# A planner's 512-column working tiles raised from 40 to 47, in room taken from the DMA scratch

## The chip, the cores and the metric

The kernel runs on one core of one Trainium2 chip. The time is the device time of one execution in microseconds. Before the change three runs took 2082.89, 2094.52 and 2097.59 us, a median of 2094.52 us.

## The reference

Two models run one after the other, all in float32, batch 1 and model width 1024, on 256 tokens.

The first model has two layers and a context of 256 further tokens. Each layer begins with a modulation: a vector `silu(c) @ ada_w + ada_b` of six parts that shift, scale and gate. The even layer (layer 0) mixes with multi-head attention of eight heads beside gated linear attention in chunks of 64. The odd layer (layer 1) mixes with a gated delta network of eight heads: chunks of 64 tokens, forward and backward, and in each chunk a triangular system is solved.

```
a_mat = jnp.where(strict, jnp.einsum('bhnid,bhnjd->bhnij', kb, k) * decay, 0.0) + jnp.eye(C)
sol = lax.linalg.triangular_solve(a_mat, rhs, left_side=True, lower=True)
...
s = s * ge_c[..., None, None] + jnp.einsum('bhcd,bhcv->bhdv', ke_c, v_new)
```

After each mixer comes an MLP with squared ReLU, of inner width 4096. The second model has two hybrid layers (sparse attention over a chosen set of keys, beside an mLSTM), each followed by a gated MLP of inner width 2816. It is modulated in the same way, from `w_mod`.

## The kernel before

Activations lie in SBUF as tiles with 128 of the model's columns on the partitions and the tokens along the row. Every dense product is done three times on TensorE: the weights and the activations are split into a high part and a low rest, and high by high, high by low and low by high are added in PSUM. Weights come in pieces of 128x1024 (512 KB, eight blocks of 128x128) through `Stream.piece` (line 694): one DMA from SP's queue into `wraw` (4 buffers), then `whi` by ScalarE or VectorE and `wlo` always by VectorE (3 buffers each). A dense product of 512 columns over the model width is 24 matmuls, one piece. Modulation weights come as `mraw` (512 KB each, 4 buffers); a group of eight program matmuls `modps` (16 in the trace, since each makes two passes) uses two of them.

The order of all instructions is not the order of the code. The class `Program` records every operation with the tiles that it reads and writes, and `schedule` (line 460) then plays the engines forward with costs written in the class, and hands each engine the operation of the highest priority that is ready. An operation that opens a tile may start only when its group of tiles has a free slot: `fits` (line 516) asks `Slots.room` (line 242), and this also keeps slots back for tiles that earlier operations will need. Four groups hold the working tiles, by their length in columns, and the last one, of 512 columns (2 KB on each partition), has `H2` slots:

```
for size, bufs in ((4, 64), (64, 24), (256, self.H1), (512, self.H2)):
    if n <= size:
        return self.nc.tile(self.act, shape, dtype, name, f"t{size}", bufs)
```

So `H2` bounds how far the plan can run ahead in any layer. Where TensorE would have nothing to do, or only narrow matmuls, the planner puts in matmuls `filled`, which compute nothing that is used (lines 416 and 591 to 608). They are the only instructions whose number depends on the plan. Some operations may go to either of two engines, and the planner chooses.

The constants `cst` of a layer are loaded into 512-column slots too (`load_consts`, line 757; `cst_1130`, `1132`, `1133` for layer 1, `cst_2230`, `2231`, `2232` for the second model) and hold them until their last use.

Layer 1 is the place that the prediction speaks of most. In `odd_layer` (line 1224) it holds the normalised input, split, in 16 slots of 512 columns (`xnh`, `xnl`), keys in 8 (`kT`, `kN`), queries in 2 and values in 8 (`vN`). A value product (eight of them) passes through `conv3`, which takes up to three slots more (`cy`, `cc`, `ce`), and then four transposes `vT`. Beside it `gdn_inverse` (line 1567) brings the triangular matrices (`N`) through DRAM (`gscr`) into a tile `inv`, inverts half blocks there by a recursion of 30 steps on VectorE (`invt`, `inv`), and writes them to DRAM again (`inv<-inv`). `gdn_rows` (line 1630) reads them back as `YY`, and with its first matmul, `iw`, the scan over the chunks begins.

Of the kernel before, what the change touches and what calls it, by code (L numbers as in the profile page):

```python
# [714 lines left out]
class Kernel:  # L715
# [3 lines left out]
    CV, CQ = range(6), ()  # L719
    PINP = range(4)  # L720
    EARLY = (1500, 1000, 500, 300)
    H2, H1, H0 = 40, 12, 4

    def __init__(self, tc, A, out, vat, cat):
        self.tc, self.nc, self.A, self.out, self.vat, self.cat = tc, Program(tc), A, out, vat, cat
# [1402 lines left out]
```

## Time and profile before

| | |
|---|---|
| median of three runs | 2094.52 us |
| the profiled execution | 2076.82 us |
| its span, first to last instruction | 2074.9 us |
| TensorE busy | 1994.3 us, 96% |
| weight loads busy | 1660.5 us, 80% |
| VectorE busy | 1440.4 us, 69% |
| ScalarE busy | 777.2 us, 37% |
| GpSimd busy | 261.3 us, 13% |
| mean granted clock of TensorE | 0.99 |
| moved by DMA | 328.16 MB, mean 158 GB/s |

The profile is of one execution. Busy time counts overlapping instructions of an engine once; matmuls are pipelined and their ends are modelled. A wait is put down to the event that came last before the waiting instruction started.

### The profile page before, as it was taken

The numbers are of one execution on the slowest core, as the hardware profiler recorded it, in microseconds if no ns is written. First come the engines' busy times: TensorE is split into PE (matmuls) and PEld (weight loads), VectorE is DVE, ScalarE is ACT, GpSimd is POOL, SyncE is SP. The second block draws the span as 40 slices with busy tenths as digits, with TensorE's granted clock in tenths as the row PEclk, the third lists the DMA queues.
The fourth block names the chain that finished last, engine by engine and source line by source line (L and its number), as shares of the span: only waits on it lengthen the run. The fifth ranks groups of instructions, "written<-read, shape, count | busy, mean of one in ns | idle before, by whom it ended". The sixth has DMA issues, their size and how long they took to land.

```text
span 2074.9 us, 37880 instructions
## 1 busy us (share of the span) xinstructions
PE 1994.3 (96%) x15248; PEld 1660.5 (80%) x15248; DVE 1440.4 (69%) x2959; ACT 777.2 (37%) x1594; POOL 261.3 (13%) x253
## 2 busy tenths in 40 slices
PE   7999999999999999799999999999999989989998
PEld 4766647888888778467889997787899968779998
DVE  5437655655555577757477888987887778878775
ACT  4134552301102266133253225564543155655431
POOL 1001002100000220006121103101200050021001
PEclk9999999999999999899999999999999999999999
DMA  8574103333333427777256567554666633424663
GB/s 326 197 282 141 42 31 127 118 90 96 99 99 95 159 77 159 243 261 215 60 175 208 176 187 259 195 182 157 228 184 186 214 112 108 137 82 150 183 186 102
DMA packets 108444, 328.16 MB, mean 158 GB/s; under 512 B 27211, under 2 KB 28491, under 8 KB 108140
## 3 DMA queue, kind: packets, MB, share of 16 engines
q1 hardware_dynamic: 108268, 325.73, 49.4%
q8 instruction: 120, 1.97, 0.4%
q14 instruction: 56, 0.46, 0.1%
HBM read 320.45 MB, written 5.24 MB: 157 GB/s over the span
## 4 chain that ended last, share of the span: by engine, by line
PE 85%; DVE 6%; ACT 3%; DMA 3%; issue 1%; POOL 0%; DVEq 0%; ACTq 0%; POOLq 0%
PE ps L684 66%; PE modps L684 3%; DMA mraw<-in_mod_dram 3%; PE filled L684 2%; PE po L684 1%; PE sc L684 1%; DVE acc L684 1%; ACT ny L684 1%; DVE fy L684 1%; PE ss L684 1%; PE glao L684 1%; PE as L684 1%; PE gdno L684 1%; PE pt L684 1%; PE ao L684 1%
## 5 line engine op out<-in xcount | busy, mean ns | idle before, releaser
L684 DVE TENSOR_TENSOR wlo<-wraw,whi 128x512 fp32r<-128x512 f32 x796 | 544.4, 713 | 45.7 <-ACT whi L684 34.6
L684 PE MATMUL ps<-xnh,whi 128*128 128x256 f32 (+1 forms) x1696 | 471.1, 317 | 9.4 <-ACT whi L684 3.5
L684 PE MATMUL ps<-xnl,whi 128*128 128x256 f32 (+1 forms) x1696 | 468.9, 316 | 1.2 <-POOL xnl L684 0.6
L684 PE MATMUL ps<-xnh,wlo 128*128 128x256 f32 (+1 forms) x1696 | 469.3, 316 | 0.1
L684 DVE CAST whi<-wraw 128x1024 fp32r<-128x1024 f32 x225 | 155.7, 696 | 346.9 <-PE ps L684 346.3
L684 PEld LDWEIGHTS ps<-xnh,whi 128*128 128x128 f32 x1696 | 302.8, 190 | 41.8 <-issue 6.3
L684 PEld LDWEIGHTS ps<-xnl,whi 128*128 128x128 f32 x1696 | 302.9, 191 | 26.6 <-issue 4.7
L684 PEld LDWEIGHTS ps<-xnh,wlo 128*128 128x128 f32 x1696 | 303.4, 191 | 25.8 <-issue 5.2
L684 ACT ACTIVATE whi<-wraw 128x1024 fp32r<-128x1024 f32 x173 | 182.6, 1058 | 358.1 <-PE ps L684 333.9
L684 POOL TENSOR_TENSOR sq<-sq 128x256 f32<-128x256 f32 (+1 forms) x53 | 56.4, 1064 | 829.6 <-ACT sq L684 769.5
L684 PE MATMUL ps<-mh,wlo 128*128 128x512 f32 (+1 forms) x512 | 139.7, 336 | 0.0
L684 PE MATMUL ps<-mh,whi 128*128 128x512 f32 (+1 forms) x512 | 139.6, 336 | 0.0
L684 PE MATMUL ps<-ml,whi 128*128 128x512 f32 (+1 forms) x512 | 139.1, 336 | 0.0
L684 PE MATMUL filled<-fill 128*128 128x512 f32 x414 | 128.9, 436 | 0.0
L684 PE MATMUL modps<-mraw,cst 128*32 128x256 f32 x1408 | 98.2, 396 | 22.0 <-DMA mraw<-in_mod_dram 12.3
L684 PEld LDWEIGHTS ps<-ml,whi 128*128 128x128 f32 x512 | 89.7, 190 | 10.2 <-DVE ml L684 0.2
L684 PEld LDWEIGHTS ps<-mh,wlo 128*128 128x128 f32 x512 | 89.8, 190 | 9.9
L684 PEld LDWEIGHTS ps<-mh,whi 128*128 128x128 f32 x512 | 89.8, 190 | 10.0
L684 PEld LDWEIGHTS filled<-fill 128*128 128x128 f32 x414 | 76.1, 200 | 26.9 <-issue 13.7
L684 PEld LDWEIGHTS modps<-mraw,cst 128*32 128x32 f32 x1408 | 36.8, 110 | 66.0 <-DMA mraw<-in_mod_dram 21.8
L684 PE MATMUL ps<-fh,whi 128*128 128x256 f32 x352 | 88.3, 284 | 0.0
L684 PE MATMUL ps<-fh,wlo 128*128 128x256 f32 x352 | 87.8, 285 | 0.1
(513 smaller groups left out, 3398.5 us busy)
## 6 DMA issues: line engine op xcount, KB each, us to landing
mraw<-in_mod_dram SPq DMA_DIRECT2D x192, 512.0 KB
wraw<-in_mlp_dram SPq DMA_DIRECT2D x128, 512.0 KB
wraw<-in_gu_dram SPq DMA_DIRECT2D x88, 512.0 KB
wraw<-in_hin_dram SPq DMA_DIRECT2D x54, 512.0 KB
wraw<-in_dn_dram SPq DMA_DIRECT2D x44, 512.0 KB
wraw<-in_oin_dram SPq DMA_DIRECT2D x25, 512.0 KB
wraw<-in_ein_dram SPq DMA_DIRECT2D x18, 512.0 KB
wraw<-in_hout_dram SPq DMA_DIRECT2D x16, 512.0 KB
```

Of the source, the lines that this page charges most:

```text
L684: getattr(self.real[op.eng], method)(*a, **kw)
```

## The change

Two numbers are changed. The program object is made with a DMA scratch of 1 KB on each partition in place of the 16 KB that it has by default, and the seven more slots of 512 columns (14 KB on each partition) go into that room.

```diff
-    H2, H1, H0 = 40, 12, 4
+    H2, H1, H0 = 47, 12, 4
...
-    nc = bacc.Bacc("TRN2", target_bir_lowering=False, num_devices=1)
+    nc = bacc.Bacc("TRN2", target_bir_lowering=False, num_devices=1, dynamic_dma_scratch_size=1024)
```

No operation of the computation is added or removed. The order changes on every engine, since the planner has other slots to give. TensorE's program holds 12244 rows other than fillers both times, and 414 fillers before, 351 now. Counted at the same landmarks of TensorE's program, the fillers up to each are:

| up to the first | before | now |
|---|---|---|
| `logit` (layer 0's gates, end of the first stage) | 23 | 30 |
| `ab` (layer 1's gates) | 81 | 82 |
| `iw` (layer 1's scan) | 172 | 130 |
| dense product of layer 1's output (`oh`) | 230 | 189 |
| `ki` of the first hybrid layer | 254 | 218 |
| `ki` of the second hybrid layer | 335 | 274 |
| end | 414 | 351 |

GpSimd's program grows from 258 to 267 instructions, ScalarE's shrinks from 1532 to 1525 and VectorE's from 2910 to 2908. SP has 671 both times.

The first place is TensorE in layer 1, at the recursion: `qk` and `gT` belong to the scan's preparation, `ps` with 128x512 are dense products for the values, and the recursion itself runs on VectorE beside these rows. Before:

```order
L684 MATMUL filled<-fill 128x512 x11
L684 MATMUL ps<-xnh,whi 128x512
L684 MATMUL ps<-xnl,whi 128x512
L684 MATMUL ps<-xnh,whi 128x512
L684 MATMUL ps<-xnl,whi 128x512
L684 MATMUL filled<-fill 128x512 x11
L684 MATMUL modps<-mraw,cst 32x256 x8
L684 MATMUL filled<-fill 128x512 x3
L684 MATMUL modpt<-cst_80,modsb 128x128 x2
L684 MATMUL modps<-mraw,cst 32x256 x8
L684 MATMUL filled<-fill 128x512 x6
L684 MATMUL modps<-mraw,cst 32x256 x8
```

And now:

```order
L684 MATMUL beR<-be,cst_1131 64x8 x4
L684 MATMUL filled<-fill 128x512 x2
L684 MATMUL ps<-xnh,whi 128x256
L684 MATMUL ps<-xnl,whi 128x256
L684 MATMUL qk<-qT,kT 64x64 x16
L684 MATMUL modps<-mraw,cst 32x256 x8
L684 MATMUL filled<-fill 128x512 x4
L684 MATMUL modpt<-cst_80,modsb 128x128 x2
L684 MATMUL filled<-fill 128x512 x5
L684 MATMUL modps<-mraw,cst 32x256 x8
L684 MATMUL filled<-fill 128x512 x6
L684 MATMUL modps<-mraw,cst 32x256 x8
```

What moved are the value products. Before, 92 of their 128x512 matmuls stand behind the last group `modps` with fillers around it, and now 22; the other 70 stand ahead of the rows shown. Between that group and the first `iw` stood 22 fillers and 12 groups `modps`; now no filler and two groups. By `iw` the plan has run 45 groups in place of 50, by `gdno` (the scan's output) 46 in place of 55. The rest is made up later: between the second hybrid layer's beginning (the last `fh` matmul) and its `ki` stand 10 groups in place of 4.

The second place is SP's queue there (`gscr` takes a matrix to DRAM, `inv<-gscr` brings a half of one back in another layout, `wraw<-in_oin` is a weight piece of layer 1). Before:

```order
L684 DMA wraw<-in_oin_dram 128x1024 x5
L684 DMA gscr<-N 128x512 x2
L684 DMA inv<-gscr 8x64x64 x4
L684 DMA gscr<-N 128x512 x6
L684 DMA wraw<-in_oin_dram 128x1024
L684 DMA inv<-gscr 8x64x64 x12
L684 DMA wraw<-in_oin_dram 128x1024 x4
L684 DMA mraw<-in_mod_dram 128x1024 x16
L684 DMA inv_1333<-inv 64x4096
L684 DMA inv_1332<-inv 64x4096
```

And now:

```order
L684 DMA gscr<-N 128x512 x3
L684 DMA inv<-gscr 8x64x64 x4
L684 DMA gscr<-N 128x512
L684 DMA inv<-gscr 8x64x64 x4
L684 DMA gscr<-N 128x512 x4
L684 DMA wraw<-in_oin_dram 128x1024 x4
L684 DMA inv<-gscr 8x64x64 x8
L684 DMA wraw<-in_oin_dram 128x1024 x2
L684 DMA mraw<-in_mod_dram 128x1024 x2
L684 DMA wraw<-in_oin_dram 128x1024 x2
L684 DMA mraw<-in_mod_dram 128x1024 x2
```

Eight of the sixteen `inv<-gscr` are issued earlier, and four weight pieces stand ahead of the last eight in place of one ahead of the last twelve. Further on, the first `YY` was issued behind six pieces of `oout`, and mod pieces between them; it now follows right behind five pieces of `oin` and four of `oout`.

The third place is SP's queue at the beginning of the program, as a difference:

```order
+L684 DMA cst_1130<-in_cst_dram 128x512
 L684 DMA cst_1131<-in_cst_dram 128x66
-L684 DMA mraw<-in_mod_dram 128x1024 x4
+L684 DMA cst_1132<-in_cst_dram 128x512
+L684 DMA cst_1133<-in_cst_dram 128x512
+L684 DMA cst_2230<-in_cst_dram 128x512
+L684 DMA mraw<-in_mod_dram 128x1024 x2
+L684 DMA cst_2231<-in_cst_dram 128x512
+L684 DMA cst_2232<-in_cst_dram 128x512
+L684 DMA mraw<-in_mod_dram 128x1024 x2
```

Six constants of later layers, 256 KB each, are loaded in the first stage, four of them ahead of modulation pieces that layer 0 begins with. They hold six of the 47 slots from there on; before, four of them were loaded at the end of layer 0's mixer, and two at the end of layer 1's.

## Rows read from the trace of the kernel before

**Rows 1.** The page's head and section 1, whole span: busy us, share, instructions.

```profile
span 2074.9 us, 37880 instructions
...
PE 1994.3 (96%) x15248; PEld 1660.5 (80%) x15248; DVE 1440.4 (69%) x2959; ACT 777.2 (37%) x1594; POOL 261.3 (13%) x253
```

**Rows 2.** Busy time by stretch, all engines: stretch, length, engines' busy (count), clock, DMA, GB/s.

```profile
0.00:50.00 50.00, 35.80 (x335) 23.91 (x336) 27.93 (x63) 23.74 (x45) 8.30 (x9) 1.00 0.89 325
450.00:500.00 50.00, 50.00 (x223) 41.37 (x222) 30.91 (x49) 11.30 (x17) 0.00 (x0) 1.00 0.32 95
820.50:859.80 39.30, 29.94 (x271) 18.77 (x267) 37.43 (x142) 10.81 (x23) 3.00 (x4) 0.91 0.66 240
859.80:945.50 85.70, 74.79 (x616) 55.12 (x616) 47.57 (x84) 32.57 (x81) 11.26 (x11) 0.96 0.85 276
945.50:1024.00 78.50, 76.57 (x2038) 63.33 (x2035) 46.34 (x88) 22.64 (x50) 32.07 (x33) 1.00 0.45 136
1651.60:1693.00 41.40, 34.90 (x242) 25.95 (x240) 29.11 (x51) 19.15 (x46) 19.61 (x25) 0.92 0.44 149
```

**Rows 3.** Costliest groups of the page (its section 5): count, busy us, mean ns, idle before.

```profile
L684 PE MATMUL filled<-fill 128*128 128x512 f32 x414 | 128.9, 436 | 0.0
L684 PE MATMUL modps<-mraw,cst 128*32 128x256 f32 x1408 | 98.2, 396 | 22.0 <-DMA mraw<-in_mod_dram 12.3
```

**Rows 4.** Busy time by stretch of the filler matmuls alone, columns as in Rows 2.

```profile
0.00:736.80 736.80, 28.39 (x81) 16.15 (x81) 1.00 0.41 135
736.80:820.50 83.70, 6.32 (x18) 2.98 (x18) 1.00 0.52 97
820.50:859.80 39.30, 15.32 (x51) 9.73 (x51) 0.91 0.66 240
859.80:945.50 85.70, 6.94 (x22) 3.69 (x22) 0.96 0.85 276
945.50:1045.00 99.50, 17.74 (x58) 9.63 (x58) 1.00 0.38 118
```

**Rows 5.** Instructions on tile inv: count, ns min/median/max, first and last start.

```profile
L684 DVE TENSOR_TENSOR invt<-inv x60: 178/342/739, 828.2 to 857.5; 128x30 f32<-128x30 f32 x4, 128x58 f32<-128x58 f32 x4, 128x84 f32<-128x84 f32 x4, 128x108 f32<-128x108 f32 x4
...
L684 SPq DMA_DIRECT2D inv<-gscr x16: 281/2045/3771, 775.4 to 813.0; - x16
L684 SPq DMA_DIRECT2D YY<-inv x16: 579/626/842, 934.5 to 996.6; - x16
```

**Rows 6.** Timeline of TensorE at 835 us: start, length, instruction, idle before and releaser.

```profile
835.26 0.38 PE L684 MATMUL modpt<-cst,modsb 128*128 128x128 f32 x2
842.46 0.65 PE L684 MATMUL modps<-mraw,cst 128*32 128x256 f32 x4 [6.82 <-DVE mod L684]
```

**Rows 7.** Chain that ended last, 815 to 950 us: start, length, what.

```profile
818.61 8.81 DMA mraw<-in_mod_dram
...
848.32 4.32 DMA mraw<-in_mod_dram
...
853.38 5.73 DMA mraw<-in_mod_dram
...
866.35 12.71 DMA mraw<-in_mod_dram
```

**Rows 8.** Waits of TensorE, 820 to 946 us: us in total, times, longest.

```profile
PE modps L684 <- DVE mod L684: 7.9, 2, 6.8
PE modps L684 <- DMA mraw<-in_mod_dram: 6.9, 4, 5.8
```

**Rows 9.** Chain over the whole span, a piece of 512-column dense matmuls.

```profile
63.85 34.71 PE ps L684 x153
```

**Rows 10.** Busy time by stretch, all engines, four stretches of 7 us.

```profile
835.00:842.00 7.00, 0.64 (x4) 0.28 (x2) 6.97 (x23) 0.00 (x0) 0.74 (x1) 0.88 0.44 150
842.00:849.00 7.00, 6.54 (x42) 3.52 (x43) 6.46 (x23) 0.00 (x0) 0.83 (x1) 0.63 0.49 157
871.00:878.00 7.00, 1.20 (x11) 0.66 (x11) 1.38 (x3) 1.39 (x2) 0.00 (x0) 0.75 0.99 349
878.00:885.00 7.00, 6.81 (x37) 4.22 (x34) 4.51 (x9) 4.84 (x11) 0.00 (x0) 0.76 1.02 400
```

**Rows 11.** Idle time of TensorE ahead of modps: releaser, us in total, times.

```profile
  DMA mraw<-in_mod_dram: 34.1, 31
```

**Rows 12.** Timeline of SP's DMA issues, 770 to 862 us.

```profile
773.29 0.93 SPq L684 DMA_DIRECT2D gscr<-N  x2
775.37 3.92 SPq L684 DMA_DIRECT2D inv<-gscr  x4
779.39 5.31 SPq L684 DMA_DIRECT2D gscr<-N  x6
788.87 0.33 SPq L684 DMA_DIRECT2D wraw<-in_oin_dram  x1
789.30 25.38 SPq L684 DMA_DIRECT2D inv<-gscr  x12
814.78 2.86 SPq L684 DMA_DIRECT2D wraw<-in_oin_dram  x4
818.61 39.02 SPq L684 DMA_DIRECT2D mraw<-in_mod_dram  x16
860.21 1.17 SPq L684 DMA_DIRECT2D inv<-inv  x2
```

**Rows 13.** Waits of SP's queue, 737 to 960 us: us in total, times, longest.

```profile
SPq L684 <- DVE wlo L684: 49.4, 12, 13.5
```

**Rows 14.** Instructions on tile iw, columns as in Rows 5.

```profile
L684 PE MATMUL iw<-YY,N x256: 184/191/212, 943.8 to 1006.3; 32*32 32x32 f32 x128
```

**Rows 15.** DMA queues of the page (its section 3): packets, MB, share of 16 engines.

```profile
q1 hardware_dynamic: 108268, 325.73, 49.4%
q8 instruction: 120, 1.97, 0.4%
q14 instruction: 56, 0.46, 0.1%
```

## The prediction

> **What bounds the kernel now.** I read the page's busy shares first. TensorE is busy for 1994.3 of 2074.9 us, so 80.6 us are idle; no other engine passes 69% but its own weight loads, which run beside it [rows 1]. Next the busy time by stretch, to see where the idle time lies: in an MLP there is none (50.00 of 50.00 us), while the 125.0 us of layer 1 from 820.50 to 945.50 hold 9.36 + 10.91 = 20.3 us [rows 2]. Third the fillers: 414 of them are busy for 128.9 us, 0.311 us each, and inside "busy" [rows 3]. So TensorE could be shorter by at most 80.6 + 128.9 us, and both parts lie in the mixers. In the two stretches of layer 1 stand 73 fillers, 22.3 us [rows 4].
>
> Last, what ends the waits there. From 828.2 to 857.5 us VectorE runs the recursion [rows 5]. TensorE has little to do beside it, and waits 6.82 us for a modulation vector that VectorE writes between two steps [rows 6]. Then, on the chain that ended last, come modulation pieces in flight: 8.81, 4.32, 5.73 and 12.71 us [rows 7]; DMA is 85% busy behind the recursion, at 276 GB/s [rows 2].
>
> The code says why TensorE is short of work there. At the recursion the input (16), keys (8), queries (2) and values (8) hold 34 slots, and constants held 4 of 40: 2 free, and 6 until the second half of the values is opened. A value product wants three. With 47 slots and six constants in them the same count leaves 7, and 11. The order shows the effect: 70 matmuls of 512 columns now stand ahead of the recursion's last mod group.
>
> **The change part by part.** The real work of TensorE is the same, 12244 rows, so the end moves by fillers, by idle time and by clock.
>
> *Fillers.* 63 fewer, at 0.311 us [rows 3]: -19.6 us. By place: 1 more ahead of `ab`, 43 fewer from there to `iw`, 6 more from there to the first `ki`, 25 fewer to the second one's, 2 fewer behind it. If each had stood beside a wait that stays, removing them would be worth 0; I take the whole, since TensorE is the chain nearly everywhere.
>
> *Idle time in layer 1.* Bounds 0 and -20.3 us [rows 2]. 7.9 us are waits for `mod` behind the recursion, and they stay, for two mod banks still end there; 6.9 us are direct waits for `mraw`, and these lose their cause, since two mod groups in place of twelve stand between the recursion and `iw` [rows 8]. I take half, -10.
>
> A second way to the same number: the stretch of 85.7 us loses 70 matmuls at 34.71/153 = 0.227 us [rows 9], 15.9 us; 22 fillers, 6.9 us [rows 4]; and ten mod groups of 16 passes at 98.2/1408 us, 1.1 us each [rows 3], 11 us. That leaves 52 us, 10.9 of them the old idle time. What is only moved comes up elsewhere, under the recursion or later, so this is no second gain; it shows what would fill the idle time.
>
> *Mod groups paid later.* Six more stand between the last `fh` and `ki` of the second hybrid layer, 41.4 us long with 6.5 idle [rows 2]. Their matmuls are in the real work already. Their pieces, 12 of 512 KB, may come late: TensorE lost 34.1 us to `mraw` over 1408/16 = 88 groups [rows 3, 11], 0.39 us each, so six cost 2.3 us. Bounds 0, as DMA is 44% busy there [rows 2], and 12.7, the longest such wait [rows 7]. I take +2.3.
>
> *Constants in the first stage.* Four of 256 KB are now queued ahead of modulation pieces, where DMA is 89% busy at 325 GB/s [rows 2]: 1.05 MB take 3.2 us. The first stage's seven extra fillers (23 to 30 up to `logit`) carry 2.2 us of this in the sum already, so +1.0. Bounds 0 and, with the two further constants, 4.8 - 2.2 = 2.6.
>
> *SP's queue at the recursion.* Eight of sixteen `inv<-gscr` go early, and the last eight stand behind four weight loads. An `inv<-gscr` of the twelve takes 25.38/12 = 2.1 us of the queue [rows 12]; four fewer behind the last `gscr` save 8.5 us. A load on this queue waited 49.4/12 = 4.1 us for a buffer [rows 13]; four cost 16.5. Bounds -8.5 and +8.0 for the recursion's start; I take 0. Behind SP's queue wait the recursion and, through it, `YY` and the scan.
>
> *YY behind nine weight loads.* SP reached the `inv<-inv` at 860.21 [rows 12]. Nine loads at 4.1 us end at about 898, and the first `iw` came 9.3 us after the first `YY` (943.8 against 934.5 [rows 5, 14]). So the scan could begin at about 907. TensorE's own work reaches 860 + 41 to 52 = 901 to 912. The two meet, and I add nothing.
>
> *Other engines.* Nine more instructions on GpSimd and nine fewer on ScalarE and VectorE lie under TensorE (13, 37 and 69% busy [rows 1]): 0. *The scratch.* All of the program's own transfers are issued by SP on the hardware queue; GpSimd issues none [rows 15]. Whether that queue uses the scratch no row shows; I take 0 and keep the other case as a rival. The Trainium skill (DMA: Bandwidth & Descriptors, Terms) says that software-generated descriptors lie in rings in SBUF and that hardware generation hands them straight to the DMA engines. By that rule the cut is free, and the sum stays as it is; no run here shows where the descriptors lie.
>
> Sum: -19.6 - 10 + 2.3 + 1.0 = -26.3 us. The profiled execution took 2076.82 us, 1.9 of them around its span, so it would be 2050.5. The median of the runs is 17.7 us above that execution; I set the difference against the median: 2094.5 - 26.3 = 2068.2. The forecast's own range goes from -44 (all 20.3 us of idle time, two slow-clock dips gone) to -8 (idle time kept, both late bounds in part).
>
> **Rivals.** One per cent, about what a measurement of this kernel can tell from no change, is 20.9 us: faster is below 2073.6, slower above 2115.4.
>
> *The idle time only moves.* The fillers go, and TensorE waits elsewhere as long as before. For it: much of the idle time here hangs on VectorE's recursion. Against it: rows 7 blame loads that the new order spreads out. -19.6 + 3.3: 2078, within 1%. 16%.
>
> *The scan starts no earlier.* If the nine loads ahead of `YY` wait 8 us each, twice the mean [rows 13], `YY` stays at 934 and layer 1 gains nothing. The 20 fillers elsewhere remain: -6.2 + 3.3, 2092. For it: nine buffers have to come free first. Against it: five of the nine are the pieces that TensorE is using at that point. 10%.
>
> *The clock falls for want of fillers.* After 6.36 idle us from 835 to 842 the granted clock over the next 7 us is 0.63, which is 74% of them at 1.2 GHz; after 5.80 idle us from 871, two stretches show 0.75 and 0.76 [rows 10]. Such a dip costs some 3 us. Four new ones in thinner stretches give 2080, within 1%. For it: each drop follows 7 us in which TensorE was busy for 0.64 and 1.20 us, and fillers are taken out of such places. Against it: what stands there now in layer 1 is dense work. 8%. The Trainium skill (TensorE: Matmul & The Clock Gate, Part 1) calls the slow clock the default and activity what lifts it; by that rule taking fillers away speaks against the change, and the trace agrees as far as both drops follow idle time.
>
> *The recursion starts late: slower.* The four loads ahead of the last eight `inv<-gscr` wait for buffers that dense products release. At the longest wait, 13.5 us each [rows 13], the recursion starts 54 - 8.5 = 45.5 us late. TensorE runs out of dense work under it, so the 10 us of idle time are not won: 2094.5 - 16.3 + 45.5 = 2124. It is slower than before from 6.2 us a load on, against a mean of 4.1. For it: rows 13 has one such wait. Against it: eight transfers are out of the way earlier. 4% for over 1%.
>
> *The scratch bounds the transfers in flight.* Then DMA slows where it is nearly full, 0.89 x 50 us in the first stage and 0.85 x 85.7 us in layer 1 [rows 2], 117 us together; at half the rate the time is 2094.5 + 117 - 26 = 2185. It decides from the point where fewer than today's transfers fit. Against it: no transfer is issued by GpSimd, and 325.73 of 328.2 MB go by the hardware queue [rows 15]. 3%.
>
> **How the numbers follow.** The forecast has 59%, 56 of them beyond 1%. Faster: 0.56. Same: 3 + 16 + 10 + 8 = 0.37. Slower: 4 + 3 = 0.07. The range 2050 to 2092 leaves out the slower 7%, part of the second rival and the tails of the forecast.
>
> **What would show it.** Fillers near 351, busy about 109 us. TensorE's idle time from the recursion to the first `iw` about half of 20 us, and that `iw` some 35 us closer to the recursion's end. The recursion starting no more than 8 us later after the last `gscr`. No new `mraw` wait above 6 us ahead of the second `ki`. DMA rates in the first stage unchanged. I would be wrong if idle time appears ahead of `iw`, if the recursion slips, or if clocks below 0.9 show up in the hybrid layers.

## The result: 1.2% faster, at the ratio forecast

Four runs of each kernel gave 2057.41 us now and 2088.7 us before, a ratio of 0.988 [0.9841, 0.9918]; in six later runs it was 0.989 [0.985, 0.9929]. The forecast was 2068.2 against 2094.5, 0.987. All ratios and median clocks below are of fast runs; of all runs only two, both with 41 slots (2106.73 and 2108.45 us), were in the slow state. The profiled execution of the change took 2053.38 us. The first group below is its page's head and section 1, the second its two groups of section 5.

```profile
span 2051.6 us, 37725 instructions
...
PE 1969.5 (96%) x15185; PEld 1647.4 (80%) x15185; DVE 1450.6 (71%) x2957; ACT 771.1 (38%) x1587; POOL 269.9 (13%) x262
```

```profile
L684 PE MATMUL modps<-mraw,cst 128*32 128x256 f32 x1408 | 98.1, 393 | 14.9 <-DMA mraw<-in_mod_dram 11.1
L684 PE MATMUL filled<-fill 128*128 128x512 f32 x351 | 108.2, 431 | 0.0
```

Against [rows 1, 3] the span is 23.3 us shorter. Fillers are 20.7 us less, the rest of TensorE's busy time is 4.1 us less (1865.4 to 1861.3), and its idle time is 1.5 us more (80.6 to 82.1). By stretch, from one landmark of TensorE's program to the next:

| up to | before, us | now | difference | idle | fillers, us |
|---|---|---|---|---|---|
| first `logit` | 159.2 | 164.0 | +4.8 | 14.2 to 18.1 | 9.9 to 10.5 |
| `ab` | 577.6 | 581.6 | +4.0 | 5.9 to 6.7 | 18.4 to 17.8 |
| recursion | 91.4 | 99.6 | +8.2 | 1.0 to 0.9 | 8.4 to 3.4 |
| its end | 29.3 | 30.2 | +0.9 | 8.5 to 4.6 | 12.6 to 11.1 |
| first `iw` | 86.3 | 46.1 | -40.2 | 11.4 to 6.8 | 7.5 to 0.7 |
| first `gdno` | 79.7 | 80.6 | +0.9 | 1.9 to 4.0 | 16.6 to 17.7 |
| first `ki` | 265.7 | 271.3 | +5.6 | 5.2 to 7.7 | 9.3 to 9.2 |
| last `ki` | 405.8 | 401.2 | -4.6 | 13.4 to 12.6 | 24.3 to 16.8 |
| end | 379.9 | 377.0 | -2.9 | 19.2 to 20.7 | 21.8 to 20.9 |

The gain is one stretch, from the recursion's end to `iw`. All engines in it, first before, then now (columns as in [rows 2]):

```profile
857.50:943.80 86.30, 74.93 (x587) 54.72 (x585) 48.12 (x90) 33.47 (x79) 9.55 (x9) 0.96 0.84 277
```

```profile
875.40:921.50 46.10, 39.34 (x317) 34.61 (x318) 33.44 (x64) 26.90 (x65) 10.23 (x10) 0.93 0.71 206
```

Busy time of the dense products alone (tile `ps`) shows why; columns are the stretch, its length, then busy time of TensorE, weight loads, VectorE and ScalarE, clock, DMA and GB/s. First before, from `ab` to the recursion and from its end to `iw`; then the same two now.

```profile
736.80:828.20 91.40, 54.21 (x253) 40.41 (x252) 11.02 (x18) 7.73 (x14) 1.00 0.56 122
857.50:943.80 86.30, 50.53 (x284) 41.10 (x284) 5.64 (x11) 6.42 (x14) 0.96 0.84 277
```

```profile
745.60:845.20 99.60, 70.12 (x317) 51.93 (x316) 13.12 (x21) 8.04 (x14) 1.00 0.67 156
875.40:921.50 46.10, 31.54 (x212) 29.19 (x212) 5.90 (x11) 3.77 (x9) 0.93 0.71 206
```

15.9 us of dense products moved from behind the recursion to ahead of it, the figure that the prediction worked out from 70 matmuls. SP's timeline of the change (start, length, issue, count) then shows the recursion's two ends and the first `YY`:

```profile
785.55 3.82 SPq L684 DMA_DIRECT2D gscr<-N  x3
790.64 3.58 SPq L684 DMA_DIRECT2D inv<-gscr  x4
794.32 2.46 SPq L684 DMA_DIRECT2D gscr<-N  x1
796.83 8.97 SPq L684 DMA_DIRECT2D inv<-gscr  x4
805.89 3.93 SPq L684 DMA_DIRECT2D gscr<-N  x4
809.91 4.79 SPq L684 DMA_DIRECT2D wraw<-in_oin_dram  x4
814.75 17.89 SPq L684 DMA_DIRECT2D inv<-gscr  x8
...
878.08 1.16 SPq L684 DMA_DIRECT2D inv<-inv  x2
879.33 4.78 SPq L684 DMA_DIRECT2D mraw<-in_mod_dram  x2
884.16 15.27 SPq L684 DMA_DIRECT2D wraw<-in_oin_dram  x5
901.21 9.12 SPq L684 DMA_DIRECT2D wraw<-in_oout_dram  x4
912.45 11.46 SPq L684 DMA_DIRECT2D YY<-inv  x8
```

The last `gscr` leaves at 809.8 and the recursion starts at 845.2, 35.4 us later; before it was 784.7 and 828.2, 43.5 us [rows 5, 12]. Behind the last `gscr` the new queue thus saves 8.1 us, but that `gscr` itself comes 16.3 us later after `ab`. VectorE's timeline tells where most of this is from: the last matrices `N`, before and then now.

```profile
782.28 1.29 DVE L684 TENSOR_TENSOR N<-N,nbe 128x512 f32<-128x512 f32 x2
```

```profile
794.79 1.29 DVE L684 TENSOR_TENSOR N<-N,nbe 128x512 f32<-128x512 f32 x2
```

They are done 46.8 and 50.5 us after `ab`, 3.7 us later now. Before, the last `gscr` left 1.1 us behind them, and now 13.7: the second group of `inv<-gscr` (796.83) stands ahead of the last four `gscr` on the queue. So the queue's own effect is 12.6 - 8.1 = +4.5 us, and with the 3.7 the recursion starts 8.2 us later.

TensorE waits less from the recursion's start to `iw`. Its longest causes of waiting now (us in total, times, longest), against 7.9 us for `mod` and 6.9 for `mraw` in [rows 8], and 0.8 for `cy`:

```profile
PE vT L684 <- DVE cy L684: 5.5, 1, 5.5
PE modps L684 <- DVE mod L684: 2.7, 1, 2.7
PE modps L684 <- DMA mraw<-in_mod_dram: 1.7, 3, 0.9
```

From 34.4 us, the time from `inv<-inv` to `YY`, 24.4 go to nine weight pieces (before: 74.3 us, with 14 weight and 23 modulation pieces).

### The profile page after: what moved, and what is told of

Same layout as the page of the kernel before. It is cut to its first block, busy times and chain, and to the rows that moved or that the text cites. A ratio compares the mean times of both kernels' runs of the same rounds, so it can differ in the third digit from the quotient of the medians.

```text
span 2051.6 us, 37725 instructions
## 1 busy us (share of the span) xinstructions
PE 1969.5 (96%) x15185; PEld 1647.4 (80%) x15185; DVE 1450.6 (71%) x2957; ACT 771.1 (38%) x1587; POOL 269.9 (13%) x262
## 4 chain that ended last, share of the span: by engine, by line
PE 85%; DVE 6%; DMA 4%; ACT 3%; issue 1%; POOL 0%; SPq 0%; DVEq 0%; ACTq 0%; POOLq 0%
PE ps L684 67%; DMA mraw<-in_mod_dram 3%; PE modps L684 3%; PE filled L684 2%; PE sc L684 1%; PE po L684 1%; DVE acc L684 1%; PE ss L684 1%; ACT ny L684 1%; PE glao L684 1%; PE gdno L684 1%; PE pt L684 1%; PE MS L684 1%; DVE fy L684 1%; DVE wlo L684 1%
## 5 line engine op out<-in xcount | busy, mean ns | idle before, releaser
L684 DVE TENSOR_TENSOR wlo<-wraw,whi 128x512 fp32r<-128x512 f32 x796 | 547.2, 716 | 29.1 <-ACT whi L684 18.4
L684 PE MATMUL ps<-xnh,whi 128*128 128x256 f32 (+1 forms) x1696 | 448.7, 317 | 9.4 <-ACT xnh L684 4.9
L684 PE MATMUL ps<-xnh,wlo 128*128 128x256 f32 (+1 forms) x1696 | 448.9, 317 | 5.3 <-DVE wlo L684 5.2
L684 PE MATMUL ps<-xnl,whi 128*128 128x256 f32 (+1 forms) x1696 | 447.5, 316 | 0.0
L684 PEld LDWEIGHTS ps<-xnh,whi 128*128 128x128 f32 x1696 | 295.3, 191 | 37.2 <-ACT xnh L684 6.3
L684 PEld LDWEIGHTS ps<-xnh,wlo 128*128 128x128 f32 x1696 | 295.6, 191 | 30.2 <-DVE wlo L684 6.9
L684 PEld LDWEIGHTS ps<-xnl,whi 128*128 128x128 f32 x1696 | 295.1, 191 | 25.0 <-issue 5.8
L684 PE MATMUL ps<-mh,wlo 128*128 128x512 f32 (+1 forms) x512 | 146.9, 336 | 0.0
L684 PE MATMUL ps<-ml,whi 128*128 128x512 f32 (+1 forms) x512 | 146.5, 336 | 0.0
L684 PE MATMUL modps<-mraw,cst 128*32 128x256 f32 x1408 | 98.1, 393 | 14.9 <-DMA mraw<-in_mod_dram 11.1
L684 PE MATMUL filled<-fill 128*128 128x512 f32 x351 | 108.2, 431 | 0.0
L684 PE MATMUL ps<-fl,whi 128*128 128x256 f32 x352 | 89.2, 283 | 0.0
```

Source lines behind the costliest of these rows:

```text
L684: getattr(self.real[op.eng], method)(*a, **kw)
```

## The experiments

Unless told otherwise each ratio is to the kernel before on the same chip. In the table "ahead" is dense work of tile `ps` from `ab` to the recursion, "pieces" the modulation pieces on SP's queue between `inv<-inv` and `YY`, "to `iw`" the time from the recursion's end to `iw`; these and the idle time are from one profile each, the clock is the median of the runs.

| kernel | fillers | ahead, us | pieces | to `iw`, us | idle, us | clock | ratio |
|---|---|---|---|---|---|---|---|
| before (40) | 414 | 54.2 | 23 | 86.3 | 80.6 | 0.987 | 1 |
| 40, scratch 1 KB | 414 | 54.2 | 23 | 86.4 | 83.0 | 0.988 | 1.0003 |
| 41 slots | 353 | 59.7 | 18 | 75.3 | 88.5 | 0.980 | 0.9997 |
| 44 slots | 346 | 61.8 | 12 | 66.1 | 88.0 | 0.978 | 1.0008 |
| 46 slots | 434 | 59.6 | 35 | 103.7 | 98.0 | 0.980 | 1.0141 |
| 47 slots, again | 351 | 70.1 | 2 | 45.6 | 79.6 | 0.984 | 0.989 |
| 48 slots | 402 | 59.7 | 34 | 101.3 | 103.4 | 0.977 | 1.0165 |
| 47, five held in layer 1 | 347 | 59.5 | 16 | 66.9 | 89.8 | 0.978 | 1.0004 |
| 40, pieces behind `YY` | 369 | 54.2 | 2 | 71.6 | 86.4 | 0.981 | 1.0027 |
| 46, pieces behind `YY` | 439 | 59.7 | 0 | 100.5 | 108.3 | 0.973 | 1.0245 |
| 47, pieces behind `YY` | 357 | 70.1 | 0 | 40.5 | 82.9 | 0.985 | 0.9951 |
| 47, constants later | 351 | 70.0 | 2 | 46.0 | 82.4 | 0.984 | 0.9904 |
| 40, no fillers | 0 | 54.3 | 23 | 86.0 | 140.3 | 0.945 | 1.0047 |

**The scratch alone.**

Against the kernel before:

```diff
-    nc = bacc.Bacc("TRN2", target_bir_lowering=False, num_devices=1)
+    nc = bacc.Bacc("TRN2", target_bir_lowering=False, num_devices=1, dynamic_dma_scratch_size=1024)
```

> 40 slots as before, the scratch alone cut to 1 KB. All five engines get the same instructions in the same order as before, so only the scratch differs. Theory (the scratch is not used by these transfers): ratio 1.000 to the kernel before, inside 0.995 to 1.005, DMA in the first 50 us still near 0.89 busy. Rival (the scratch bounds transfers in flight): slower wherever DMA is nearly full, up to +117 us, 1.056. Second rival (a smaller scratch is itself worth the gain): 0.988.

Measured 1.0003 [0.9985, 1.0021], and over the first 50 us (columns as in [rows 2]):

```profile
0.00:50.00 50.00, 33.98 (x339) 23.12 (x340) 28.06 (x63) 24.27 (x47) 8.31 (x9) 0.93 0.91 331
```

DMA is 91% busy at 331 GB/s. The smaller scratch costs nothing and gains nothing; that rival is out. The rule of the Trainium skill (DMA: Bandwidth & Descriptors, Terms) that the prediction cited would have it so; no run shows where the descriptors lie.

**41, 44 and 46 slots.** The change with another number:

```diff
-    H2, H1, H0 = 47, 12, 4
+    H2, H1, H0 = 41, 12, 4
```

> 1 KB scratch, 41 slots: one of the seven. The plan has 353 fillers (47 slots: 351, 40 slots: 414), 125 of them up to the first iw, and 20 modulation groups between the gates and iw where 47 slots have 12 and 40 have 21. Theory of the prediction (free slots let the value products run ahead, and more slots give more): a seventh of 31 us, 4 us, 0.998. Rival (what counts is the plan that comes out, told by its fillers at 0.311 us each, whatever the number of slots): 61 fewer, -19 us, 0.991.

> 1 KB scratch, 44 slots. The plan has 346 fillers, the fewest, and 25 of them up to the first logit, where 47 slots have 30. Theory of the prediction (slots): four sevenths of 31 us, 18 us, 0.9915. Rival (the plan's fillers): 68 fewer, -21 us, 0.990. The two hardly differ here; if constants ahead of the first modulation pieces cost 47 slots 5 us, this kernel is below 47 slots, at 2052 us.

> 1 KB scratch, 46 slots, one fewer than the change. The plan has 434 fillers, 20 more than before, 183 of them up to iw. Theory of the prediction (slots): six sevenths of 31 us, 27 us, 0.987. Rival (the plan's fillers): +6 us, 1.003. These lie 1.6% apart, so this kernel tells most.

Measured 0.9997 [0.9967, 1.0028], 1.0008 [0.9981, 1.0035] and 1.0141 [1.0112, 1.0169]. Both theories fail. With 41 slots alone that of the slots could still stand, since its 0.998 lies in the interval. But slots don't do it by their number, for 46 are slower than 40. Fillers don't either: 61 and 68 fewer bring nothing. In those two kernels 12.0 and 16.8 us of fillers are gone (116.9 and 112.1 us left), but idle time is 7.9 and 7.4 us longer, and the median clock is 0.980 and 0.978 against 0.987. What the clock is worth is seen in the kernel before: of its 29 runs beside these the quickest took 2073.88 us at 0.992, the slowest 2096.39 at 0.977, 1.5 us for each thousandth (a line through all runs of a set gives 1.1 to 2.0 in the three sets); seven and nine thousandths are then an estimated 10 and 14 us. So two rivals of the prediction, the idle time that only moves and the clock that falls, hold there together. From `ab` to `iw` these two kernels do win 12.4 and 11.1 us (194.6 and 195.9 against 207.0); it is lost elsewhere.

The stretch to `iw` seemed to follow the modulation pieces ahead of `YY` (2, 12, 18, 23, 35 pieces: 46, 66, 75, 86, 104 us). That became a theory of its own, Q, and the next four kernels test it.

**Modulation pieces behind `YY`, at 40, 46 and 47 slots; and layer 1 held back.** The edit of the first three:

```diff
+            behind = nc.behind
+            if l == 2:
+                nc.behind = self.yy
             for k, raw in zip(ks, raws):
                 nc.sync.dma_start(raw, self.A[f"mod{l}"][j * 8 + k])
+            nc.behind = behind
...
+            if not hasattr(self, "yy"):
+                self.yy = nc.ops[-1].i
```

and of the fourth, at 47 slots, where `hold` opens five tiles of 512 columns with a copy of one column and `free` writes one column of each at the scan's end:

```diff
         si = Stream(self, "oin")
+        self.held = self.hold(5, xn[7][1][:, 511:512].bitcast(F32))
...
             ys.append((c, y))
+        self.free(self.held, ys[3][1][:, 0:1])
```

> 40 slots and the scratch of before; the modulation pieces of the second model's first layer may only be issued once the first YY is. On SP's queue 2 of them stand between the inv<-inv and the first YY, where before had 23 (47 slots: 2), and 13 weight pieces (14; 9). Theory Q (the end of layer 1's mixer is set by how many modulation pieces SP's in-order queue carries ahead of YY; slots only change that number): from the recursion's end to iw 52 us in place of 86 (from 46, 66, 75, 86 and 104 us at 2, 12, 18, 23 and 35 pieces: 1.53 us a piece, 1.8 a weight piece), fillers 414 to 369, and the kernel gains 14 to 28 us with no slot added: 0.987 to 0.993. Rival (the slots themselves are what gains): the stretch stays above 75 us, ratio 0.998 or more.

> 46 slots, 1 KB, the same order to SP: no modulation piece ahead of YY in place of 35, 13 weight pieces. The plan has 439 fillers (46 slots alone: 434). Theory Q: from the recursion's end to iw 50 us in place of 104; of the 54 us some 22 are twenty modulation groups that are only put off, so 32 are won: 1.0141 becomes 0.999. Rival (time follows the fillers of the plan): 5 more, 1.015 as before. Rival (TensorE's own work ahead of iw sets it, 116 fillers and 9 groups in place of 88 and 29): the stretch shrinks by 13 us only, and the total stays at 1.01.

> The change with the same order to SP: no modulation piece ahead of YY in place of 2, 8 weight pieces in place of 9, 357 fillers in place of 351. Theory Q: hardly anything is left to take, from the recursion's end to iw 41 in place of 46 us, the total 0.987 to 0.990 as the change. Rival (the change's gain is a chance of its one plan, and any other order of modulation pieces loses it): 0.995 or more.

> 47 slots, but five of them are taken by idle tiles from layer 1's normalised input to the scan's end, so that layer 1 has two free slots again as before, with the constants loaded early as in the change. The plan has 347 fillers (the change 351), 16 modulation pieces and 12 weight pieces ahead of YY. Theory Q and the prediction's (free slots in layer 1 are what matters): from the recursion's end to iw 72 us, and the total like 41 and 44 slots, 0.998 to 1.002. Rival (fillers, or slots in the other layers): 0.987 to 0.989.

Measured 1.0027 [1.0004, 1.0051], 1.0245 [1.0219, 1.027], 0.9951 [0.9928, 0.9973] and 1.0004 [0.9976, 1.0032]. Q falls with 46 slots: not one piece stands ahead of `YY`, and the stretch is 100.5 us in place of 103.7, where Q had 50. All engines, from the recursion's end to `iw`, with 46 slots and then with 46 slots and pieces behind `YY`:

```profile
870.70:974.40 103.70, 85.88 (x700) 60.60 (x702) 48.02 (x98) 28.21 (x62) 9.99 (x11) 0.95 0.82 286
```

```profile
867.60:968.10 100.50, 73.91 (x394) 59.87 (x393) 45.99 (x88) 25.67 (x56) 8.26 (x9) 0.90 0.33 93
```

DMA is 33% busy in place of 82, and TensorE waits 26.6 us in place of 17.8. Its timeline in the second kernel (start, length, instruction, idle before and releaser) shows for what:

```profile
876.71 2.66 PE L684 MATMUL filled<-fill 128*128 128x512 f32 x11
883.50 0.72 PE L684 MATMUL vT<-cst,cy 128*128 128x128 f32 x4 [4.13 <-DVE cy L684]
885.36 0.79 PE L684 MATMUL ps<-xnh,whi 128*128 128x512 f32 x1 [1.15 <-ACT vN L684]
...
893.50 2.66 PE L684 MATMUL filled<-fill 128*128 128x512 f32 x11
900.16 0.66 PE L684 MATMUL vT<-cst,cy 128*128 128x128 f32 x4 [4.00 <-DVE cy L684]
```

The value products left behind the recursion go one at a time: 24 matmuls, 11 fillers, a wait of 4 us for the convolution `cy`, four transposes, the next product; 16.7 us for each (883.50 to 900.16). With 46 slots alone modulation groups stand in such a gap (32 and twice 8 of their matmuls from 913.01 to 919.28), and the wait for `cy` is 0.31 us there. In the change's plan this piece of TensorE's program looks different:

```profile
878.36 0.50 PE L684 MATMUL ps<-xnh,wlo 128*128 128x512 f32 x1 [1.23 <-DVE wlo L684]
...
881.44 0.51 PE L684 MATMUL ps<-xnh,whi 128*128 128x256 f32 x2
...
883.56 0.60 PE L684 MATMUL vT<-cst,cy 128*128 128x128 f32 x4
...
885.18 0.40 PE L684 MATMUL ps<-xnh,whi 128*128 128x256 f32 x2
...
885.89 0.60 PE L684 MATMUL vT<-cst,cy 128*128 128x128 f32 x4
...
897.60 1.12 PE L684 MATMUL vT<-cst,cy 128*128 128x128 f32 x4 [5.48 <-DVE cy L684]
```

Dense products of 256 columns, the output gates, stand between the value products and their transposes, and the transposes of two products follow each other within 2.3 us (883.56, 885.89). The last product is not covered: its transposes wait 5.48 us for `cy`, most of what TensorE is idle in this stretch.

With five slots held, the change does 59.5 us of dense work ahead of the recursion in place of 70.1, and its gain is gone. The edit takes back one thing, the free slots of layer 1 (the planner then orders everything anew), and 347 fillers, fewer than the change has, don't save it. Its profile and that of the change run again are at nearly the same clock (0.984 and 0.983) and lie 11.9 us apart; from `ab` to `iw` it takes 188.4 us in place of 175.4, so at that clock the loss is in layer 1. The medians lie further apart, with clocks of 0.978 and 0.984. At 40 slots the pieces behind `YY` shorten the stretch by 14.7 us, and nothing is left of it at the end: putting modulation groups off is no gain by itself. At 47 the dense work stays ahead and the stretch is even shorter (40.5 us), but the ratio of 0.9951 is that of the rival (0.995 or more), and not of Q: 52 groups are done by the first `ki` in place of 59, and from there to the last `ki` it takes 416.7 us in place of 401.2. So both seem to belong to the change's plan: dense work ahead of the recursion, and groups left over in a number that later stretches can take. The second is read from this one kernel; no run moves the value products alone and leaves the rest of the order as it was.

**Constants later, no fillers, 48 slots, and the change again.** In the first, six loads are moved after the order is made, and no other instruction:

```diff
+    STAGE1 = 64
...
         order = self.schedule()
+        src = lambda op: op.forms["SP"][1][1].tensor.name if op.eng == "SP" else ""
+        moved = [op for op in order if src(op) in [f"in_cst{i}_dram" for i in (2, 4, 5, 6, 7, 8)]]
+        order = [op for op in order if op not in moved]
+        last = [n for n, op in enumerate(order) if src(op).startswith("in_mod")][self.STAGE1 - 1]
+        order[last + 1:last + 1] = moved
```

The second, on the kernel before:

```diff
             for op in order:
+                if op is self.idle[0]:
+                    continue
```

The third has 48 for 47, the fourth no edit.

> The change, with six loads moved on SP's queue and nothing else: the constants of layer 1 and of the second model go behind the 64th modulation piece, at the end of layer 0's mixer, and all other instructions of all engines keep their order. Theory C (these 1.5 MB ahead of the first modulation pieces cost what layer 0's gates are later by, 159.2 to 164.0 us, where the prediction took 1.0): the first logit again at 159 to 160, the total 4 to 5 us below the change beside it. Rival (TensorE is held there by something else, or the time comes back before layer 1): the first logit at 164, or at 160 with the total unchanged.

> The kernel before with its 414 fillers left out and every other instruction in its old order; they compute nothing that is used. Theory D (the prediction's price of a filler, 0.311 us each, holds: TensorE is the chain, so a filler taken away is time won): -129 us, 0.94. Rival (fillers stand mostly in waits that stay, and hold the clock): idle time grows by most of 129 us, the granted clock falls below the 0.986 of before, the total moves by less than 1%, or is longer.

> 1 KB scratch, 48 slots, one more than the change. In the plan 278 dense matmuls stand ahead of the fillers beside the recursion; 47 slots have 328, 41 to 46 slots 276 to 284, before 256. 34 modulation pieces stand ahead of YY (47 slots: 2), and there are 402 fillers. Theory of the prediction in its simple form (more slots, more gain): 0.987 or less. Theory E (the gain is the dense work that a plan brings ahead of the recursion and the modulation groups that it leaves behind; only the plan of 47 slots does it): like 43 to 46 slots, from recursion's end to iw 90 to 105 us, ratio 1.00 to 1.015.

> The change itself, for comparison on the same chip as the others: 0.988, from recursion's end to iw 46 us, two modulation pieces ahead of YY.

Constants later: 0.9904 [0.9875, 0.9934], not below the change's 0.989 [0.985, 0.9929], and the first `logit` at 167.2 us, where the change beside it has 169.0 (and 164.0 in its first profile: one order differs by 5 us between executions) and the order of before has 158.5 to 159.2. Theory C fails; the bytes of the constants are not what delays the first stage. TensorE's order seems to be. First the order of before (the kernel with the small scratch alone), then constants later:

```profile
19.94 4.78 PE L684 MATMUL filled<-fill 128*128 128x512 f32 x11
24.66 0.41 PE L684 MATMUL modq<-mraw,cst 128*32 128x128 f32 x4
25.94 1.07 PE L684 MATMUL modq<-mraw,cst 128*32 128x128 f32 x28 [0.87 <-DMA mraw<-in_mod_dram]
```

```profile
19.65 5.80 PE L690 MATMUL filled<-fill 128*128 128x512 f32 x14
28.86 1.65 PE L690 MATMUL ps<-xnh,whi 128*128 128x512 f32 x3 [3.41 <-ACT xnh L690]
30.44 1.94 PE L690 MATMUL modq<-mraw,cst 128*32 128x128 f32 x32
```

The plan, which has the constants ahead of the modulation pieces, puts a dense product, which waits for `xnh`, ahead of the group that uses these pieces. Their four buffers come free that much later, and SP's next sixteen pieces wait for these, as the two queues show, before and then constants later:

```profile
26.87 28.70 SPq L684 DMA_DIRECT2D mraw<-in_mod_dram  x16
```

```profile
32.40 31.30 SPq L690 DMA_DIRECT2D mraw<-in_mod_dram  x16
```

The difference is 5.5 us; in the change itself they are first issued at 32.38. That the order alone makes it was read from these rows, and not tried by moving the group.

No fillers: 1.0047 [1.0013, 1.0082], slower. Its page and its recursion, from 846.5 to 876.6 us:

```profile
span 2107.2 us, 37052 instructions
...
PE 1966.9 (93%) x14834; PEld 1637.5 (78%) x14834; DVE 1439.0 (68%) x2959; ACT 777.0 (37%) x1594; POOL 260.7 (12%) x253
```

```profile
846.50:876.60 30.10, 15.29 (x108) 4.69 (x112) 28.86 (x118) 3.54 (x5) 1.57 (x2) 0.54 0.70 248
```

128.9 us of fillers are gone; idle time is 59.7 us longer (140.3), and the other matmuls are busy for 101.5 us more (1966.9 against 1865.4), with a mean granted clock of 0.940 in this profile against 0.990 in that of before (medians of the runs: 0.945 and 0.985). By the clock alone 1865.4 us would become 1865.4 x 0.990 / 0.940 = 1965, so it accounts for nearly all of that (an estimate). In the recursion, where TensorE is left with 15.3 us of work in 30, 0.54 is granted: nearly all of it at 1.2 GHz. Theory D fails outright: a filler's busy time is not its price, and in this plan the price is below zero. These rows agree with the rule of the Trainium skill (TensorE: Matmul & The Clock Gate, Part 1), by which activity lifts the clock.

48 slots: 1.0165 [1.0119, 1.021], with 101.3 us from the recursion's end to `iw`, as E said, and a ratio a little above its 1.00 to 1.015; all engines in that stretch:

```profile
873.70:975.00 101.30, 84.85 (x667) 60.70 (x666) 48.09 (x99) 27.50 (x60) 11.34 (x12) 0.92 0.87 285
```

Of all the kernels run none is faster than the change.

## Why the prediction held, and where its steps did not

*The sum: near, and partly by luck.* Between the two profiles, at clocks of 0.990 and 0.989, the time fell by 23.3 us, where -26.3 was forecast. Fillers gave -20.7 (forecast -19.6). Idle time gave +1.5, where the other three terms make -6.7. TensorE's other work gave -4.1, which the forecast had at 0 ("The real work of TensorE is the same") and no run here explains. So a miss of 8.2 us on idle time is more than half covered by the other two.

*The mechanism in layer 1: right.* Free slots let value products run ahead; 15.9 us of them did, and with five slots held back they don't, and the gain is gone. What the prediction gave as a second way to the same number was the better account: it put the stretch from the recursion to `iw` at 52 us, and 46.1 were measured. From `ab` to `iw` 31.1 us are won: fillers 28.5 to 15.2 us, idle time 20.9 to 12.3, modulation groups 24.8 to 18.6, the rest 3.0.

*Fillers, -19.6: right as a sum, wrong as a price.* They are 351 and 20.7 us shorter. But 61 and 68 fewer bring nothing in other plans, and 414 fewer make it slower. The step that said "I take the whole, since TensorE is the chain nearly everywhere" does not hold: in these kernels fewer fillers are time won only where real work takes their place, as in layer 1 and, with modulation groups, up to the last `ki`.

*Idle time, -10: near in its place, for other reasons in part, and not right in the whole.* From `ab` to `iw` it fell by 8.6 us. Waits for `mraw` fell from 6.9 to 1.7 us, as said. Those for `mod`, which were to stay at 7.9, fell to 2.7. And a wait ahead of `iw` that was not foreseen came up, 5.5 us for `cy`, where before has 0.8; idle time appearing there was one of the signs of being wrong. In the whole it came back: 3.9 us in the first stage, 2.1 in the scan, 2.5 up to the first `ki`. The whole is +1.5. The first rival, given 16%, was right in that. The time was still won, since fillers went and, in layer 1, dense work stood in their place.

*Mod groups paid later, +2.3.* The price was read wrongly. The 34.1 us of [rows 11] add up the idle time of two engines' rows: 12.3 ahead of the matmuls, as the page has it in [rows 3], and 21.8 ahead of their weight loads. By the 12.3 a group costs 0.14 us, and six cost 0.8. Measured, waits for `mraw` in the last 45 us up to the last `ki` went from 0.8 to 3.4 us, none above 0.8; so the term came out about as large as forecast, by luck. From the first to the last `ki` the kernel is 4.6 us quicker: there eight more groups took the place of 25 fillers.

*Constants in the first stage, +1.0: mis-sized, and for the wrong reason.* With 2.2 us of fillers the forecast was 3.2 us for this stage. The first `logit` is 4.8 us late in the profile compared (0.6 of it fillers, 3.9 idle time), and 8.7 and 10.5 us in the two of the last group against 158.5. The transfers don't do it; that the order made for them does is the reading above, and not tried. Of the terms this is the one most clearly wrong in its reason.

*SP's queue at the recursion, 0.* Behind the last `gscr` the lower bound came, -8.1 us. What the term left out is that the eight `inv<-gscr` that go early hold up the last four `gscr` by 12.6 us, so the queue as a whole makes the recursion later by 4.5, and `N` by 3.7. It costs TensorE little, since value products fill the time (0.9 us idle up to the recursion). They are not what delays it: the last `kk`, the matmul that `N` is made from, starts 42.4 us after `ab` before and 43.3 now.

*YY behind nine weight pieces.* The first `iw` was forecast 49 us after the recursion's end, measured 46.

*The clock.* Median 0.982 and 0.984 in the change's two sets of runs, 0.985 to 0.987 in those of before: by 1.5 us a thousandth an estimated 2 to 8 us lost. The rival is there in small, and at full size with 41 and 44 slots.

*Open:* whether the value products alone, moved within the order of before, give the gain; why the planner finds this order at 47 slots and at none of 41, 44, 46 and 48; and why the hybrid layers are slower when still more groups are left to them.

## What to carry to other kernels

A matmul put in to keep an engine busy has no price of its own: take it out only by putting real work there, and look at idle time and clock before counting it as a gain. Where an order is planned greedily, more room is another plan and not a better one, so try the neighbouring sizes, and judge by where the real work stands around the longest serial piece. Room kept for a facility that a program doesn't use can be taken at no cost, once that is measured alone.

## What was not expected of the hardware

One program's executions differ by 22.5 us with the granted clock (2073.88 us at 0.992 to 2096.39 at 0.977), about as much as this change is worth. And 414 matmuls that compute nothing, 129 us of busy time, make the kernel 0.5% quicker: left out of the same order, the real matmuls take 101.5 us longer between the two profiles (granted clock 0.990 and 0.940) and idle time grows by 59.7.
